# Gate rows in column groups, pool products in three passes, feature-major context keys: one layer of a hybrid diffusion block

## The chip, the core and the metric

The kernel runs on one core of a Trainium2 chip. The metric is device time in microseconds (us). The core has a matrix engine (TensorE, PE in the profile, with its weight loads as PEld), a vector engine (VectorE, DVE), a scalar engine (ScalarE, ACT), GpSimd (POOL) and SyncE (SP), which here issues most DMA transfers. Matrix products land in PSUM, eight banks of 128 x 512 floats, and ScalarE or VectorE carries them out.

## The reference

One layer with a model width of 1024 on 1024 latent tokens (a 16 x 64 grid) and 256 context tokens, all in float32:

```python
sh1, sc1, gt1, sh2, sc2, gt2 = split(silu(c) @ w_mod + b_mod, 6)       # 1024 each
h_x = rmsnorm(x, g_pre_mix) * (1 + sc1) + sh1                          # h_c: the same with c_ctx
u, q, k, v = split(h @ w_in)                                           # 512 each, for latent and context
d = window_mean(u, 2/4/8/16) - u                                       # 4 groups of 128 channels
pool = einsum('blgc,gcd->blgd', d, pool_w) * pool_scale
attn = neighbourhood_attention(q_x, k_x, v_x, k_c, v_c, rpb)           # 8 heads of 64
x = x + gt1 * rmsnorm(concat(pool, attn) @ w_out, g_post_mix)
y = square(relu((rmsnorm(x, g_pre_mlp) * (1 + sc2) + sh2) @ w1)) @ w2
out = x + gt2 * rmsnorm(y, g_post_mlp)
```

## The kernel before

A product of two float32 matrices is made in three passes: each operand is split into a high part in the type fp32r (a cast on ScalarE) and a low part (a subtraction on VectorE), and `three` (L167) adds high x high, high x low and low x high in one PSUM bank. A few small products run as plain fp32 matmuls instead; each of these shows as two records in the trace.

TensorE does the work in this order:

- Start: x is normalised and transposed, shift and scale rows are made for both token kinds (`mod_sums`, tile pm, 128x32 weights and 256 columns in four column groups of the array), and the keys kT of the latent tokens.
- Context keys and values: `pkc` is made by tokens (two groups of 24 matmuls with 512 columns), copied into kct, transposed in blocks of 128 (`pkct`, L542), and copied into kcT, feature by token. Then `pvc`, the context's values.
- The latent values `pv`, eight groups of 24.
- The pools' stage: for each of four channel groups two groups of 24 matmuls (`pu`), and `pooled` on VectorE: sums of doubling width in the pages sa and sb, edges in ed, and the difference d.
- The queries of the first half of the tokens (`pq`), then one query group of the second half, then `pool_out`: eight plain fp32 products `py` of d with pool_w, each written as a high and a low part into mix.
- Attention, 32 units (head pair j, column block m), in software-pipelined steps i: scores of unit i, transposes of unit i - 2 (`turn`), value products of unit i - 3 (`values`). The three other query groups lie between the first units.
- The output product (`out_sums`: po, then pw) begins in the steps i = 32 to 35 that run attention dry; then the MLP, two products in a scheme with seven block products, which takes the time from about 360 us on.

Four vectors are needed that come later: shift and scale of the MLP (sh, sc) and the two gates (a, b). Each is a sum on VectorE over eight loads of w_mod (`mod_sum`, L190: one operation of 128x1024 for a load), closed by a product with ones that adds the partitions. These steps are taken from a list by `background(n)`, called between the groups of matmuls. For the gates, `mod_gate` (L195) multiplies the sum by a ones matrix into all partitions (two matmuls of 512 columns), then by the norm's gain on VectorE, and one row goes to DRAM, from where `gate_page` spreads it later.

Memory is in pools with a fixed number of buffers: `act`, 33 pages of 4 KB a partition (tag pg), `wraw`, 4 buffers for loads of 512 KB, and `whl`, 8 buffers for high and low weights. A tile takes a buffer that an earlier tile gave free and waits for that tile's last reader. Where a block stands in `in_order(...)`, the listed engines keep the order as written; elsewhere a scheduler decides it. The start up to the context keys and the attention loop stand in such blocks.

In the attention loop `LOADS` and `HALVES` give the steps at which the output weights are loaded and split: at each entry of HALVES, `weight_split(n)` casts one 128x512 half on ScalarE, and `low()` subtracts it on VectorE in the next step.

Of the kernel before, what the change touches and what calls it, by code (L numbers as in the profile page):

```python
# [17 lines left out]
P = 128  # L18
# [61 lines left out]
def hybrid_block(ctx, tc, x, ctx_in, w_mod, b_mod, gp1, gp2, w_in, pool_w, rpb, w_out, w1, w2, vectors,  # L80
# [17 lines left out]
    def page(name, dt=F32):  # L98
        return act.tile([P, 1024], dt, tag="pg", name=name)
# [83 lines left out]
    def mod_sum(name, c, alloc, sT):  # L183
# [4 lines left out]
        for k in range(KT):  # L188
            w = load(f"wm{name}_{k}", w_mod[k * P : (k + 1) * P, c * D : (c + 1) * D])
            nc.vector.scalar_tensor_tensor(acc, w, sT[:, k : k + 1], acc, mul, add)  # L190
            yield acc

    def mod_gate(name, acc, gp, bank):
        g = load(f"gp{name}", gp.rearrange("(o d) -> o d", o=1).to_broadcast([P, D]).rearrange("p (a b) -> p a b", a=2))
        for h in range(2):  # L195
            hs = slice(h * 512, (h + 1) * 512)
            ps = bank(f"pg{name}{h}")
            nc.tensor.matmul(ps, ones, acc[:, hs], start=True, stop=True)
            nc.vector.tensor_tensor(acc[:, hs], ps, g[:, hs], mul)

    def mod_column(name, acc, bank):
        ps = bank(f"pc{name}")
# [20 lines left out]
    with tc.tile_pool(name="ps1", bufs=6, space=PSUM) as ps1, tc.tile_pool(name="tmp1", bufs=3) as tmp:  # L223
# [6 lines left out]
        def once(name, shape):  # L230
            return tmp.tile(shape, F32, tag=name, name=name, bufs=1)
# [300 lines left out]
        with tc.issue_after(last[ET.DVE]):  # L532
            background(4)
# [1 line left out]
        for i in range(2):  # L535
            ps = bank(f"pvc{i}")
            token_group(ps, wgt, ctx_tok(i))
            nc.scalar.copy(vcp[:, i * 512 : (i + 1) * 512], ps)
            background()
            pt = bank(f"pkct{i}")  # L540
            for j in range(4):
                nc.tensor.transpose(pt[:, j * P : (j + 1) * P], kct[:, i, j * P : (j + 1) * P], ident)  # L542
            nc.scalar.copy(kcp.rearrange("p (j i t) -> p i j t", j=4, i=2)[:, i],
                               pt.rearrange("p (j t) -> p j t", j=4))
        kc = kcp.rearrange("p (j t) -> p j t", j=4)

        vp = [page(f"v{i}") for i in range(4)]
        for m in range(NM):
# [48 lines left out]


        def pool_out(g):
            dv = dT[g].rearrange("p (r m c) -> p m r c", r=QR, m=NM)  # L600
            for b in range(2):
                ps = bank(f"py{g}_{b}")
                nc.tensor.matmul(ps, pwt[:, g, :], dv[:, 4 * b : 4 * b + 4], start=True, stop=True)
                mp = page(f"mix1_{g}", F32R) if b else wraw.tile([P, 1024], F32R, tag="raw", name=f"mix0_{g}")
                nc.scalar.activation(mp[:, :512], ps, AF.Identity, scale=pscol[:, g : g + 1])
                nc.vector.scalar_tensor_tensor(mp[:, 512:], ps, pscol[:, g : g + 1], mp[:, :512].bitcast(F32), mul, sub)
                mix[b][g] = mp

        for g in range(4):
            up = page(f"u{g}")  # L610
            for b in range(2):
                ps = bank(f"pu{g}_{b}")
                feature_group(ps, wgt, g * P, b, range(KT))
                nc.scalar.copy(up.rearrange("p (r m c) -> p m r c", r=QR, m=NM)[:, 4 * b : 4 * b + 4],
                                   ps.rearrange("p (m r c) -> p m r c", m=4, r=QR))
            dT.append(pooled(g, up))


        tabs, msk = [], []
# [41 lines left out]
            queries(j, 0, bank(f"pq{j}_0"), (1, 2, 3, 99)[j])  # L661
        mask_page()
        tables(0)
        queries(0, 1, bank("pq0_1"), 0)
        for g in range(4):
            pool_out(g)


    with (
# [117 lines left out]

        kks = (2, 3, 0, 1)
        raw_o, wo = {}, {}
        LOADS, HALVES = (8, 10, 17, 19), (12, 13, 14, 20, 21, 22, 28, 30)  # L790
        lows = []

        def high(src, hi, lo):
# [39 lines left out]
            nc.vector.tensor_tensor(mp1[t][:, hs], ps, G1[:, hs], mul)  # L833

        with in_order(ET.PE, ET.Activation, ET.DVE, ET.SP):
            queries(1, 1, bank("pq1_1"), 0)
            for i in range(N + 4):
                if i < N and units[i][1] == 2 and units[i][0] < 3:
                    tables(units[i][0] + 1)
# [11 lines left out]
                if i in HALVES:  # L851
                    weight_split(HALVES.index(i))
                if i < N:
                    scores(i)
                else:
# [524 lines left out]
```

## Time and profile before

| | us |
|---|---|
| median of three runs | 1060.99 (1060.98 to 1061.59) |
| the profiled execution | 1061.53 |
| its span, first to last instruction | 1059.7 |
| TensorE busy in it | 1045.5 |
| VectorE busy | 685.6 |
| ScalarE busy | 507.5 |
| GpSimd busy | 55.7 |

The mean granted clock of TensorE is 0.997. In a row of the timeline the first number is the start in us from the span's beginning, the second the duration; then engine, source line, operation, output tile <- input tiles, shape and count, and in brackets how long the engine sat idle before and what released it. A matmul's recorded duration overlaps the next one's, so the pace of a stream is read from start to start. A row of the chain of waits has start, length, and what ran.

### The profile page before, as it was taken

What the parts mean: (1) busy time and instruction counts of PE and PEld (TensorE: products, weight loads), DVE (VectorE), ACT (ScalarE), POOL (GpSimd) and SP (SyncE); (2) the same over time, 40 slices, a digit from 0 to 9 for tenths busy, and PEclk for the clock granted to TensorE, in tenths of its full rate; (3) what the DMA queues carried; (4) which work ended last, traced back from release to release, by engine and by line L of the source; (5) the groups of instructions that cost most, each with busy time, mean ns of one, the idle gap of its engine ahead of it and who ended that gap; (6) DMA issues with size and microseconds to landing.
All of it is one profiled execution on the core that took longest, in us unless ns stands there. A gap on an engine that the chain in (4) does not pass through costs nothing.

```text
span 1059.7 us, 15246 instructions
## 1 busy us (share of the span) xinstructions
PE 1045.5 (99%) x5870; PEld 856.4 (81%) x5870; DVE 685.6 (65%) x1071; ACT 507.5 (48%) x882; POOL 55.7 (5%) x109
## 2 busy tenths in 40 slices
PE   8999999999999999999999999999999999999996
PEld 6788888867878888888888888888888888888885
DVE  5536624846998225799987666664577666557586
ACT  7563021236998123886555454554553335334441
POOL 2020000030120003200000000000000000000001
PEclk9999999999999999999999999999999999999998
DMA  9906740531111605445745345345597666556556
GB/s 342 326 21 230 240 146 0 165 107 55 35 39 57 159 1 180 147 150 182 255 169 179 130 146 182 129 159 189 212 354 263 233 238 218 198 165 206 168 191 203
DMA packets 94268, 179.37 MB, mean 169 GB/s; under 512 B 6898, under 2 KB 39154, under 8 KB 94196
## 3 DMA queue, kind: packets, MB, share of 16 engines
q1 hardware_dynamic: 76644, 144.80, 41.6%
q10 hardware_dynamic: 16272, 29.40, 7.5%
q0 software_dynamic: 1280, 4.21, 1.1%
q8 instruction: 46, 0.75, 0.3%
q14 instruction: 26, 0.21, 0.1%
HBM read 140.62 MB, written 37.76 MB: 168 GB/s over the span
## 4 chain that ended last, share of the span: by engine, by line
PE 89%; ACT 4%; DVE 3%; issue 1%; DMA 1%; POOL 1%; SPq 0%; POOLq 0%; DVEq 0%; ACTq 0%
PE pk L400 4%; PE S L697 3%; PE pyv L170 3%; PE pyz L170 3%; PE pyx L170 3%; PE pyx L168 3%; PE phz L169 3%; PE phv L169 3%; PE phv L168 3%; PE phz L168 3%; PE pyz L169 3%; PE pyv L169 3%; PE pyv L168 3%; PE pyz L168 3%; PE phv L170 3%; PE phz L170 3%
## 5 line engine op out<-in xcount | busy, mean ns | idle before, releaser
L1029 ACT ACTIVATE c<-c 128x512 f32<-128x512 f32 x48 | 30.3, 631 | 59.9 <-DVE c L1142 23.3
L720 ACT ACTIVATE sp<-sp,nm 128x640 f32<-128x640 f32 (+1 forms) x64 | 51.4, 804 | 7.8 <-DVE nm L711 7.3
L711 DVE CUSTOM_DVE_ANT_0 sp<-S,tab 128x640 f32<-128x640 f32 (+1 forms) x56 | 42.8, 802 | 16.1 <-PE S L697 9.4
L144 DVE TENSOR_TENSOR wpS<-S,wpS 128x512 fp32r<-128x512 f32 x64 | 43.6, 686 | 11.9 <-ACT wpS L143 11.9
L170 PE MATMUL phx<-thB,wpA 128*128 128x512 f32 x128 | 49.9, 390 | 0.0
L168 PE MATMUL phx<-thB,wpA 128*128 128x512 f32 x128 | 49.9, 390 | 0.0
L169 PE MATMUL phx<-tlB,wpA 128*128 128x512 f32 x128 | 49.8, 389 | 0.0
L143 ACT CAST wpS<-S 128x512 fp32r<-128x512 f32 x64 | 39.2, 616 | 18.2 <-PE phy L170 7.8
L139 POOL TENSOR_TENSOR ry<-vy,nhalf 128x1 f32<-128x1 f32 x8 | 4.4, 550 | 600.7 <-DVE vy L137 600.7
L1030 ACT ACTIVATE c<-c 128x512 f32<-128x512 f32 x48 | 30.3, 631 | 8.1 <-DVE sa L1100 7.4
L1136 DVE TENSOR_TENSOR c<-phz,u 128x512 f32<-128x512 f32 x16 | 11.0, 690 | 32.2 <-PE phz L170 32.1
L170 PEld LDWEIGHTS phx<-thB,wpA 128*128 128x128 f32 x128 | 24.0, 188 | 5.2 <-DVE wpA L144 0.2
L697 PE MATMUL S<-kT,q 64*128 64x384 f32 (+1 forms) x128 | 27.8, 495 | 0.4 <-DVE nm L711 0.4
L168 PEld LDWEIGHTS phx<-thB,wpA 128*128 128x128 f32 x128 | 24.0, 188 | 5.0
L169 PEld LDWEIGHTS phx<-tlB,wpA 128*128 128x128 f32 x128 | 24.0, 188 | 4.9
L833 DVE TENSOR_TENSOR mp<-pw,Ga 128x512 f32<-128x512 f32 x14 | 9.6, 688 | 27.5 <-ACT jo L130 27.5
L773 PE MATMUL pa<-pt,v 128*64 128x128 f32 x352 | 25.9, 279 | 1.2 <-ACT px L753 0.6
L168 PE MATMUL phy<-thT,wpS 128*128 128x512 f32 x64 | 24.9, 389 | 0.0
L169 PE MATMUL phy<-tlT,wpS 128*128 128x512 f32 x64 | 24.9, 389 | 0.0
L170 PE MATMUL phy<-thT,wpS 128*128 128x512 f32 x64 | 24.9, 389 | 0.0
L168 PE MATMUL phz<-thT,wpS 128*128 128x512 f32 x64 | 24.9, 389 | 0.0
L169 PE MATMUL phz<-tlT,wpS 128*128 128x512 f32 x64 | 24.9, 389 | 0.0
(922 smaller groups left out, 3269.4 us busy)
## 6 DMA issues: line engine op xcount, KB each, us to landing
b<-in_w SPq DMA_DIRECT2D x64, 512.0 KB, 4.6
hrS<-hdS SPq DMA_DIRECT2D x32, 512.0 KB, 5.1
hrA<-hdA SPq DMA_DIRECT2D x24, 512.0 KB, 5.5
wm<-in_w_mod SPq DMA_DIRECT2D x16, 512.0 KB, 9.7
wa_0w<-in_w SPq DMA_DIRECT2D x16, 512.0 KB, 4.9
wa_1w<-in_w SPq DMA_DIRECT2D x16, 512.0 KB, 4.0
hdA<-c ACTq DMA_DIRECT2D x32, 256.0 KB, 2.1
hdS<-sa ACTq DMA_DIRECT2D x32, 256.0 KB, 4.4
```

What stands on the lines that cost most here:

```text
L143: nc.scalar.copy(hi, src)
L144: nc.vector.tensor_tensor(lo, src, hi.bitcast(F32), sub)
L168: nc.tensor.matmul(ps, ahi, bhi, start=first, stop=False, skip_group_check=more)
L169: nc.tensor.matmul(ps, ahi, blo, start=False, stop=False, skip_group_check=more)
L170: nc.tensor.matmul(ps, alo, bhi, start=False, stop=last, skip_group_check=more)
L400: nc.tensor.matmul(pks[b][j], wk(wgt, k, low, j * P, P), r, start=(k == 0 and n == 0), stop=(k == KT - 1 and n == 2))
L697: nc.tensor.matmul(S[e][:, c0 : c0 + keys.shape[1]], q[hs, cols], keys[hs], start=True, stop=True)
L711: nc.vector.tensor_tensor_reduce(out=to, in0=s, in1=bt, scale=1.0, scalar=BIG, op0=add, op1=ALU.min, accum_out=nm)
L720: nc.scalar.activation(sp, sp, AF.Exp, bias=least[i, e], scale=-1.0, accum_out=sums[i][:, e : e + 1])
L773: nc.tensor.matmul(pa[e * HD : (e + 1) * HD, cols], v[:, f : f + HD], turns[i][:, e, c] if c < 4 else fifths[i][:, :, (e + 1) * HD : (e + ...
L1029: nc.scalar.activation(r, src, AF.Relu)
L1030: nc.scalar.activation(r, r, AF.Square)
```

## The change

1. `mod_gate`: the gate's 1024 values are taken as four column groups of 256. Four fp32 matmuls with 32 columns of ones write to the four partition quarters of one bank, one VectorE operation of 128x256 applies the gain (loaded by four transfers), and four transfers on GpSimd's queue, in place of one on SyncE's, write the row to DRAM.
2. Context keys are made by features (four groups of 24 matmuls with 256 columns), straight into kcT's order; the copies into kct and the transposes go.
3. `background(2)` is called after each of the eight groups of the pools' stage, so the rest of gate a's and all of gate b's sums come before the queries, and so do their loads: SyncE's queue now has the last w_mod load of a, the eight of b, and both gains before the four query weight loads.
4. pool_w and the differences d are split into high and low parts (in the pools' stage), and the pools' products run in three passes. The order of TensorE is fixed around them.
5. The steps of the output weights' splits change.

```diff
     def mod_gate(name, acc, gp, bank):
-        g = load(f"gp{name}", gp.rearrange("(o d) -> o d", o=1).to_broadcast([P, D]).rearrange("p (a b) -> p a b", a=2))
-        for h in range(2):
-            hs = slice(h * 512, (h + 1) * 512)
-            ps = bank(f"pg{name}{h}")
-            nc.tensor.matmul(ps, ones, acc[:, hs], start=True, stop=True)
-            nc.vector.tensor_tensor(acc[:, hs], ps, g[:, hs], mul)
+        g = wraw.tile([P, 1024], F32, tag="raw", name=f"gp{name}w")[:, :256]
+        quarters = gp.rearrange("(c o f) -> c o f", c=4, o=1)
+        for c in range(4):
+            nc.sync.dma_start(g[32 * c : 32 * c + 32, :], quarters[c].to_broadcast([32, 256]))
+        ps = bank(f"pg{name}")
+        for c in range(4):
+            nc.tensor.matmul(ps[32 * c : 32 * c + 32, :256], ones[:, :32], acc[:, c * 256 : (c + 1) * 256],
+                             start=True, stop=True)
+        nc.vector.tensor_tensor(acc[:, :256], ps[:, :256], g, mul)
...
-                nc.sync.dma_start(gates[name], acc[0:1, :])
+                for c in range(4):
+                    nc.gpsimd.dma_start(gates[name][:, c * 256 : (c + 1) * 256], acc[32 * c : 32 * c + 1, :256])
...
         kcp = page("kcT")
-        kct = page("kct").rearrange("p (i f) -> p i f", i=2)
+        kc = kcp.rearrange("p (j t) -> p j t", j=4)
...
-        for i in range(2):
-            ps = bank(f"pkc{i}")
-            token_group(ps, wgt, ctx_tok(i))
-            if i:
+        for j in range(4):
+            ps = bank(f"pkc{j}")[:, :CTX]
+            for k in range(KT):
+                three(ps, wk(wgt, k, 0, j * P, P), wk(wgt, k, 1, j * P, P), *hc[k], k == 0, k == KT - 1)
+            if j == 3:
                 wgt = [high_low(f"wv{kk}", raw_v[kk]) for kk in range(KT // 2)]
-            nc.scalar.copy(kct[:, i], ps)
+            nc.scalar.copy(kc[:, j], ps)
...
-            pt = bank(f"pkct{i}")
-            for j in range(4):
-                nc.tensor.transpose(pt[:, j * P : (j + 1) * P], kct[:, i, j * P : (j + 1) * P], ident)
-            nc.scalar.copy(kcp.rearrange("p (j i t) -> p i j t", j=4, i=2)[:, i],
-                               pt.rearrange("p (j t) -> p j t", j=4))
...
+        pwh, pwl = (tmp.tile([P, 512], F32R, tag=f"pw{n}", name=f"pw{n}", bufs=1) for n in "hl")
...
-                nc.tensor.matmul(ps, pwt[:, g, :], dv[:, 4 * b : 4 * b + 4], start=True, stop=True)
+                hi, lo = dT[g][b]
+                gs = slice(g * P, (g + 1) * P)
+                three(ps, pwh[:, gs], pwl[:, gs], hi, lo, True, True)
...
+                if g == 1 and b == 0:
+                    with tc.issue_after(kept[ET.Activation]):
+                        split(pwt.rearrange("p g d -> p (g d)"), pwh, pwl)
+                background(2)
+            dv = pooled(g, up).rearrange("p (r m c) -> p m r c", r=QR, m=NM)
+            dT.append([])
+            for b in range(2):
+                d = page(f"d{g}_{b}", F32R)
+                hi, lo = d[:, :512], d[:, 512:]
+                bands = lambda t: t.rearrange("p (m r c) -> p m r c", m=4, r=QR)
+                split(dv[:, 4 * b : 4 * b + 4], bands(hi), bands(lo))
+                dT[g].append((hi, lo))
...
-        LOADS, HALVES = (8, 10, 17, 19), (12, 13, 14, 20, 21, 22, 28, 30)
+        LOADS, HALVES = (8, 10, 17, 19), (12, 14, 20, 22, 29, 32, 32, 33)
```

On VectorE the changed order around the last pooling groups is: gate b's multiply, wq0l, wq1l, the add into sb of the third pooling group, wq2l, the add into sa, wq3l. On ScalarE the four query weight casts stand before the copies of the last pool groups. The add into sb waits for four transfers of POOL's queue.

More of the change, by code (lines that the diff above doesn't have):

```diff
@@ L613, in hybrid_block @@
                 feature_group(ps, wgt, g * P, b, range(KT))
-                nc.scalar.copy(up.rearrange("p (r m c) -> p m r c", r=QR, m=NM)[:, 4 * b : 4 * b + 4],
-                                   ps.rearrange("p (m r c) -> p m r c", m=4, r=QR))
-            dT.append(pooled(g, up))
+                with in_order(ET.Activation) as kept:
+                    nc.scalar.copy(up.rearrange("p (r m c) -> p m r c", r=QR, m=NM)[:, 4 * b : 4 * b + 4],
+                                       ps.rearrange("p (m r c) -> p m r c", m=4, r=QR))
+                if g == 1 and b == 0:
[10 more added lines that the diff above has]
+                dT[g].append((hi, lo))
         tabs, msk = [], []
@@ L663, in hybrid_block @@
         tables(0)
-        queries(0, 1, bank("pq0_1"), 0)
-        for g in range(4):
-            pool_out(g)
+        with in_order(ET.PE) as pools:
+            queries(0, 1, bank("pq0_1"), 0)
+            for g in range(4):
+                pool_out(g)
     with (
@@ L835, in hybrid_block @@
         with in_order(ET.PE, ET.Activation, ET.DVE, ET.SP):
-            queries(1, 1, bank("pq1_1"), 0)
+            with tc.issue_after(pools[ET.PE]):
+                queries(1, 1, bank("pq1_1"), 0)
             for i in range(N + 4):
@@ L850, in hybrid_block @@
                     mixed_split(i // 8 - 1, 0)
-                if i in HALVES:
-                    weight_split(HALVES.index(i))
+                for n, at in enumerate(HALVES):
+                    if at == i:
+                        weight_split(n)
                 if i < N:
```

2 lines of the change are left out of this document (removed).

## The prediction, on record before the changed kernel ran

> **What bounds the kernel now.** I read the page first, then busy time by stage (the windows), then what TensorE waited for, and last the timeline of TensorE at each place that the change touches.
>
> ```profile
> span 1059.7 us, 15246 instructions
> PE 1045.5 (99%) x5870; PEld 856.4 (81%) x5870; DVE 685.6 (65%) x1071; ACT 507.5 (48%) x882; POOL 55.7 (5%) x109
> PE 89%; ACT 4%; DVE 3%; issue 1%; DMA 1%; POOL 1%; SPq 0%; POOLq 0%; DVEq 0%; ACTq 0%
> ```
>
> TensorE is 89% of the chain. By stage (us; then PE, PEld, DVE, ACT, POOL busy; granted clock, DMA share, GB/s):
>
> ```profile
> 146.65:190.20 43.55, 43.55 (x194) 36.07 (x193) 19.57 (x44) 8.85 (x13) 0.00 (x0) 1.00 0.15 48
> 190.20:233.14 42.94, 42.94 (x169) 31.24 (x168) 28.43 (x38) 9.73 (x15) 12.56 (x30) 1.00 0.50 165
> 233.14:341.70 108.56, 106.91 (x1490) 85.62 (x1489) 89.18 (x260) 89.39 (x233) 10.41 (x24) 1.00 0.12 36
> 341.70:358.45 16.75, 16.75 (x146) 13.27 (x145) 5.51 (x14) 4.57 (x13) 0.00 (x0) 1.00 0.84 240
> ```
>
> The rows are the pools' stage, the queries with the pools' products, attention, and the last units with the first output products. In the first two TensorE never stops at full clock while VectorE is about half idle. So work taken off TensorE there is time saved, and work put on VectorE and ScalarE is free until one of their results comes too late. Only attention loads all three engines, and there TensorE's recorded waits are small:
>
> ```profile
> PE pa L773 <- ACT px L753: 0.6, 3, 0.2
> PE S L697 <- DVE nm L711: 0.4, 1, 0.4
> ```
>
> The last column is the longest single wait. All stages after 233 us start from what TensorE and its helpers finished before, so a saving ahead of them moves them all.
>
> **The change, part by part.** Context keys first. TensorE's timeline:
>
> ```profile
> 76.58 0.39 PE L168 MATMUL pkc<-wk0h,hc 128*128 128x512 f32 x1
> ...
> 87.46 0.39 PE L168 MATMUL pvc<-wv0h,hc 128*128 128x512 f32 x1
> ...
> 92.90 0.60 PE L542 MATMUL pkct<-ident,kct 128*128 128x128 f32 x4
> ...
> 93.57 0.39 PE L169 MATMUL pvc<-wv0l,hc 128*128 128x512 f32 x1
> ```
>
> Between the first two rows lie 48 matmuls in 10.88 us, 0.2267 each. Four transposes and the one matmul after them take 0.67 (92.90 to 93.57), so the transposes cost 0.67 - 0.23 = 0.44, twice: 0.89. Removed: 10.88 + 0.89 = 11.77. Added: 96 matmuls with 256 moving columns in place of 512. No fp32r matmul of that width is in the trace. Its neighbours:
>
> ```profile
> 70.71 1.91 PE L460 MATMUL pct<-ident,c 128*128 128x128 f32 x16
> 72.38 0.47 PE L400 MATMUL pk<-hx,wk2h 128*128 128x512 f32 x1
> ```
> ```profile
> L204 PEld LDWEIGHTS pcsh<-ones,accsh x16: 188/192/192, 110.0 to 111.7; 128*128 128x128 f32 x16
> L204 PE MATMUL pcsh<-ones,accsh x16: 164/250/250, 110.2 to 111.8; 128*128 128x1 f32 x16
> ```
>
> Sixteen 128-wide transposes take 1.67, 0.104 each; sixteen records of a single column start from 110.2 to 111.8, 0.107 each. Both load 128x128 weights every time, so about 0.106 is the floor that a weight load leaves. A line from (128 columns, 0.104) to (512, 0.2267) gives 0.145 at 256, an upper bound if the floor does not bind alone. Half of the 512-wide row is 0.1133. I take a little over half, 0.1165, because it lies above the floor and part of 0.2267 may be fixed: 96 x 0.1165 = 11.18, a gain of 0.59 (bounds 10.2 to 13.9, a gain of 1.6 to a loss of 2.1).
>
> A rule of the Trainium skill speaks against this step: TensorE: Matmul & The Clock Gate, Part 3, "What overlaps and what doesn't", says that a weight load overlaps running matmuls only when its row groups differ; here all 128 rows are the same. By it each pair would cost load plus stream, some 0.107 + 0.107, and the 96 would take 20.5, a loss of 8.8. By that rule the 512-wide pairs would need about 0.32, and the trace has 0.2267: it disagrees.
>
> Gates. Rows of the chain, then TensorE around a product in column groups:
>
> ```profile
> 206.52 1.72 PE pga L198 x4
> 219.17 1.72 PE pgb L198 x4
> 220.89 6.87 PE py L603 x16
> ```
> ```profile
> 27.10 0.63 PE L400 MATMUL pk<-hx,wk0h 128*128 128x512 f32 x2
> 27.66 1.93 PE L351 MATMUL pm<-wm,sT 128*32 128x256 f32 x32
> 29.53 0.73 PE L400 MATMUL pk<-hx,wk0h 128*128 128x512 f32 x2
> ```
>
> Removed: 2 x 1.72 = 3.44. Added: twice four fp32 matmuls of form 128x32 weights and 256 columns, each in its own group. The L351 rows are that form in four groups: 16 matmuls in 29.53 - 27.66 = 1.87, 0.47 per round of four. Before them two pk matmuls take 0.56 rather than 0.45; I count that change of form 0.11 on both sides. So 0.68 a gate, 1.36 in all: a gain of 2.08 (2.5 with nothing for the form; 0 if a lone round does not run abreast, since four times 0.43, py's 6.87 / 16, is again 1.72).
>
> Pools' products: 16 records, 6.87, become 24 fp32r matmuls of 0.2267, 5.44: a gain of 1.43. Their evictions end later than the products, covered by the query group of 5.44 behind them.
>
> What this puts on the helpers:
>
> ```profile
> 193.44 1.28 DVE L190 SCALAR_TENSOR_TENSOR acca<-wma_7w,sx,acca 128x1024 f32<-128x1024 f32 x1
> 345.76 0.68 DVE L795 TENSOR_TENSOR mix<-f,mix 128x512 fp32r<-128x512 f32 x1
> 342.45 0.61 ACT L794 CAST mix<-f 128x512 fp32r<-128x512 f32 x1
> ```
>
> Nine sums move into the pools' stage (9 x 1.28 = 11.5), and nine splits are new (6.1 on VectorE, 5.5 on ScalarE). VectorE there goes from 19.6 to about 38 of 43.6, ScalarE from 8.9 to 14.4. It fits, but the next results to come late are the split weights:
>
> ```profile
> 185.93 1.05 ACT L143 CAST wq0h<-wq0w 128x1024 fp32r<-128x1024 f32 x1 [0.50 <-PE pu L169]
> 188.37 1.23 DVE L144 TENSOR_TENSOR wq1l<-wq1w,wq1h 128x1024 fp32r<-128x1024 f32 x1
> 191.09 1.23 DVE L144 TENSOR_TENSOR wq3l<-wq3w,wq3h 128x1024 fp32r<-128x1024 f32 x1
> 181.23 1.23 DVE L576 TENSOR_TENSOR sb<-sa 128x1021 f32<-128x1021 f32 x1
> ```
> ```profile
> acca<-in_b_mod POOLq DMA_DIRECT2D x1, 4.0 KB, 3.4
> accb<-in_b_mod POOLq DMA_DIRECT2D x1, 4.0 KB, 1.7
> 201.82 0.49 POOL L186 DMA_DIRECT2D accb<-in_b_mod  x1 [0.29 <-POOL accb L185]
> ```
> ```profile
> 78.71 0.43 DVE L180 TENSOR_TENSOR hc<-hc7t,hc 128x256 fp32r<-128x256 f32 x1 [0.48 <-ACT hc L176]
> ```
>
> The context keys meet two such edges. Their first group reads all eight hc tiles in 2.8 us instead of 5.4: the low part of hc7 is ready at 79.14 and read by the 23rd matmul, 76.58 + 22 x 0.1165 = 79.14. And the values' weights take over buffers that the last of the four groups still reads: the first is free 78 matmuls on, 85.7; cast (1.05) and subtraction (1.23) end at 88.0, and the second value matmul, 76.58 + 96 x 0.1165 + 0.23, reads it at 88.0. I put 0.1 on both (0 to 0.3).
>
> The query weights: now wq3l ends at 192.32 and is first read by the 21st matmul from 190.20 on, 194.73: 2.4 us of slack. In the changed order the last pooling group stands between: wq1l, the add sb, wq2l, the add sa, wq3l. Four times some 1.19 behind 189.60 is 194.35; the slack is 0.4. And sb takes over the page of gate b's sum, so it waits for the four row transfers that POOL now issues. The fourth pool group's last products start at 184.75 (146.65 + 7 x 5.44); gate b's product is just ahead, its multiply (128x256, as the hc row) 0.4, then four issues of about 0.5, so the last starts near 187.1 and lands 1.7 to 3.4 later, at 188.8 to 190.5, against 189.60. Behind sb wait wq2l and wq3l, and TensorE behind them: 0 to 0.5 of stall on this count. I take 0.2, with 1.2 as the upper end if the transfers share the queues with the last query weight load, which now also starts only after gate b's multiply.
>
> Last units. Casts leave units 13, 21, 28 and 30; one comes to 29 and three to 32 and 33.
>
> ```profile
> 343.73 0.32 ACT L753 COPY px<-pa 128x192 f32<-128x192 f32 x1 [0.66 <-PE pz L739]
> 344.12 0.88 PE L773 MATMUL pa<-pt,v 128*64 128x128 f32 x12
> 350.60 0.39 PE L169 MATMUL po<-wo_1l,mix 128*128 128x512 f32 x1
> ```
>
> Behind the cast at 342.45 ScalarE is free 0.66 before px. Two more casts take 1.0 to 1.2, so px and the value product behind it come 0.3 to 0.5 later. wo_1l's last half is ready about 350.6, when it is read (350.60): 0.1. I count +0.35 (0 to 0.9). What attention can gain from four casts less is bounded by its 1.0 of recorded waits; I take 0.1.
>
> Sum: -0.59 + 0.1 - 2.08 - 1.43 + 0.2 + 0.35 - 0.1 = **-3.55**. The profiled execution took 1061.53 us (its span 1059.7 and 1.8 around it), 0.54 above the median of 1060.99. From the median: **1057.4**; such a profile would have a span near 1056.
>
> **Rivals.** *Weight loads set the pace of the context keys (slower).*
>
> ```profile
> 76.58 0.19 PEld L169 LDWEIGHTS pkc<-wk0l,hc 128*128 128x128 f32 x1
> ```
>
> This load starts with the matmul ahead of it (76.58), takes 0.19, and the next matmul starts at 0.2267, right behind. If that chain is what sets 0.2267, halving the columns halves nothing: 96 x 0.2267 = 21.76, a loss of 9.99, and with the other terms (-2.96) +7.0: 1068. It decides from 0.175 a matmul on, where the other gains are gone and 2.1 lost. Against it: the pcsh loads take 192 ns as well, yet follow each other at 0.11. I give it 7%.
>
> *Query weights late.* If the gate rows land 2 to 3 us later than I count, sb holds wq2l and wq3l for that long and TensorE stops 2 to 3 us: 1059.3 to 1060.3, within the noise of no change at the end. POOL's 4 KB transfers spread from 1.7 to 3.4, which speaks for it; VectorE idling for the first cast while POOL issues speaks against. 12%. The Trainium skill, SBUF — State Buffer, "The DVE blocks DMA trap", says that POOL cannot write descriptors while VectorE runs a fast-mode copy; if that held for these subtractions the transfers would land this late. The accb transfer above, at 1.7, ran beside an idle VectorE and doesn't tell.
>
> *The column groups don't run abreast for a single round*: gates stay at 3.44 and the sum is -1.5: 1059.5. The L351 rows speak against; 5%.
>
> **Numbers.** A measurement of this kernel can tell about 0.2%, 2.1 us, from no change. The forecast case has 73% and spreads over 1055.8 to 1058.8 by its bounds; the two milder rivals 17% (1059 to 1060.3), the slow one 7%, and 3% for losses that I don't see. The range 1055.8 to 1060.2 leaves out the slow rival, the unseen and a tail. Faster: nearly all of the forecast case and a share of the mild rivals, 0.78; within 0.2%: 0.13; slower: 0.09.
>
> **What would show it.** Context-key matmuls 0.113 to 0.12 apart and no transposes; pga and pgb near 0.5 to 0.7; py's stretch 5.4; no TensorE gap over 0.5 in the query group that follows the pools; values of unit 29 delayed by under 0.5. It is wrong if the context keys take over 13.9 us, if TensorE waits more than 1.2 us for wq2l or wq3l, or if anything behind 358 us changes length.

## The result, and the profile after

| | before | changed |
|---|---|---|
| median of eight runs each, us | 1061.14 (1060.98 to 1061.59) | 1057.96 (1057.71 to 1058.13) |
| the profiled execution | 1061.53 | 1057.97 |
| its span | 1059.7 | 1056.1 |

The changed kernel is 3.18 us faster, a ratio of 0.9969 (95% interval 0.9959 to 0.9980). The forecast was 1057.4 in a range of 1055.8 to 1060.2. The first lines of the page, and then the windows of the changed kernel: context keys, context values, the pools' stage, the queries with the pools' products, attention, last units (us; then PE, PEld, DVE, ACT, POOL busy; clock, DMA share, GB/s).

```profile
span 1056.1 us, 15402 instructions
PE 1041.4 (99%) x5926; PEld 857.4 (81%) x5926; DVE 687.7 (65%) x1078; ACT 510.2 (48%) x891; POOL 59.5 (6%) x117
```
```profile
76.45:88.03 11.58, 11.58 (x97) 11.55 (x96) 2.27 (x4) 7.09 (x15) 0.00 (x0) 1.00 0.00 0
88.03:99.11 11.08, 11.08 (x51) 9.01 (x49) 8.78 (x8) 2.67 (x4) 1.44 (x2) 1.00 0.80 276
146.32:191.44 45.12, 45.12 (x209) 36.20 (x208) 29.07 (x46) 10.92 (x17) 3.82 (x8) 1.00 0.49 155
191.44:229.63 38.19, 38.19 (x169) 31.29 (x167) 21.71 (x43) 11.79 (x20) 7.21 (x19) 1.00 0.13 37
229.63:337.71 108.08, 106.56 (x1489) 85.64 (x1489) 87.41 (x258) 88.06 (x231) 14.36 (x34) 1.00 0.12 38
337.71:355.04 17.33, 17.18 (x146) 13.12 (x145) 7.21 (x16) 5.94 (x16) 0.00 (x0) 1.00 0.76 218
```

TensorE is still busy for all of the first four stages. From the first pool projection to the first scores it was 86.63 us (146.51 to 233.14) and is 83.31. Attention is 0.48 shorter (108.56 before), the last units are 0.58 longer (16.75 before). Behind them nothing moved: the first matmul of the MLP came 3.31 earlier, counted from the first context key, and that of its last product, 439 us on, also 3.31. From the last matmul's start to the end of the trace it is 8.27 us in place of 8.50; with the same code there the other traces have 8.11 to 9.03.

TensorE's timeline at the context keys: the first matmul, the only irregular step among the 96, and the context values behind them.

```profile
76.45 0.28 PE L168 MATMUL pkc<-hc,wk0h 128*128 128x256 f32 x1
...
79.08 0.37 PE L169 MATMUL pkc<-hc,wk3h 128*128 128x256 f32 x1
79.29 0.28 PE L170 MATMUL pkc<-hc,wk3l 128*128 128x256 f32 x1
...
88.03 0.39 PE L168 MATMUL pvc<-wv0h,hc 128*128 128x512 f32 x1
88.31 0.50 PE L169 MATMUL pvc<-wv0l,hc 128*128 128x512 f32 x1
88.65 0.39 PE L170 MATMUL pvc<-wv0h,hc 128*128 128x512 f32 x1
```

From 79.29 to 88.03 there are 73 matmuls, 0.1197 each. The matmul at 79.08 takes 0.21 to the next: it read hc7's low part, the wait that was counted. The first two context values take 0.28 and 0.34 in place of 0.2267, the wait for wv0l. Now the gate's product and the pools' products:

```profile
156.97 0.39 PE L170 MATMUL pu<-hx,wu3l 128*128 128x512 f32 x1
157.29 0.64 PE L201 MATMUL pga<-acca,ones 128*32 128x256 f32 x8
157.86 0.50 PE L168 MATMUL pu<-hx,wu0h 128*128 128x512 f32 x1
158.20 0.39 PE L169 MATMUL pu<-hx,wu0h 128*128 128x512 f32 x1
...
218.66 0.39 PE L168 MATMUL py<-d,pwh 128*128 128x512 f32 x1
...
224.10 0.39 PE L168 MATMUL pq<-hx,wq0h 128*128 128x512 f32 x1
```

The gate takes 0.57 for its eight records, and the steps on its two sides 0.32 and 0.34 in place of 0.2267, so 0.57 + 0.09 + 0.11 = 0.78. The 24 products of the pools take 5.44, without a gap.

### The profile page after: what moved, and what is told of

It is laid out like the page before. It is cut to its first block, busy times and chain, and to the rows that moved or that the text cites. A ratio compares the mean times of both kernels' runs of the same rounds, so it can differ in the third digit from the quotient of the medians.

```text
span 1056.1 us, 15402 instructions
## 1 busy us (share of the span) xinstructions
PE 1041.4 (99%) x5926; PEld 857.4 (81%) x5926; DVE 687.7 (65%) x1078; ACT 510.2 (48%) x891; POOL 59.5 (6%) x117
## 4 chain that ended last, share of the span: by engine, by line
PE 82%; issue 11%; ACT 3%; DVE 2%; POOL 1%; DMA 1%; SPq 0%; POOLq 0%; DVEq 0%; ACTq 0%
PE pk L404 4%; PE pyv L169 3%; PE pyv L168 3%; PE pyz L169 3%; PE pyz L168 3%; PE pyx L169 3%; PE phv L170 3%; PE phz L170 3%; PE pyx L170 3%; PE phv L168 3%; PE phz L168 3%; PE phv L169 3%; PE phz L169 3%; PE pyx L168 3%; PE pyv L170 3%
```

## The experiments

Each is the changed kernel with one edit. "Against before" is the median less that of the kernel before in the same comparison (1061.83, 1061.45, 1061.63 and 1061.56 us in the four); the changed kernel's is -3.18.

| run | median us | against before | ratio (95% interval) |
|---|---|---|---|
| keys_by_tokens | 1058.64 | -3.19 | 0.9971 (0.9961 to 0.9982) |
| keys_in_pairs | 1058.25 | -3.20 | 0.9968 (0.9956 to 0.9981) |
| gates_whole | 1060.01 | -1.82 | 0.9983 (0.9974 to 0.9992) |
| gates_one_strip | 1060.84 | -0.61 | 0.9997 (0.9988 to 1.0006) |
| pools_plain | 1060.24 | -1.59 | 0.9985 (0.9977 to 0.9994) |
| sums_in_queries | 1078.75 | +17.30 | 1.0161 (1.0147 to 1.0174) |
| plain_sums_in_queries | 1060.44 | -1.19 | 0.9991 (0.9981 to 1.0000) |
| sums_in_queries_own | 1066.86 | +5.30 | 1.0051 (1.0034 to 1.0068) |
| rows_on_sync | 1058.64 | -2.99 | 0.9972 (0.9961 to 0.9982) |
| casts_as_before | 1057.80 | -4.03 | 0.9963 (0.9949 to 0.9977) |
| casts_spread | 1058.49 | -2.96 | 0.9974 (0.9965 to 0.9983) |
| pairs_casts_28_29 | 1058.03 | -3.60 | 0.9967 (0.9955 to 0.9980) |

The intervals are some 2 us wide. For edits of a few tenths I read stage lengths from the traces: in kernels that are the same up to the first context key, that matmul started anywhere from 76.45 to 78.01 us, but up to the first scores, and again in the last units, the same stretch of the same code repeats within 0.05. Attention does not: in the ten traces with the changed kernel's attention it lasts 107.82 to 108.37, so there I read single units.

**Context keys.** keys_by_tokens puts the `token_group` loop, kct and the transposes back. keys_in_pairs keeps the features-first form:

```diff
-        for j in range(4):
-            ps = bank(f"pkc{j}")[:, :CTX]
+        for js in ((0, 1), (2, 3)):
+            pss = [bank(f"pkc{j}")[:, :CTX] for j in js]
             for k in range(KT):
-                three(ps, wk(wgt, k, 0, j * P, P), wk(wgt, k, 1, j * P, P), *hc[k], k == 0, k == KT - 1)
+                for ps, j in zip(pss, js):
+                    three(ps, wk(wgt, k, 0, j * P, P), wk(wgt, k, 1, j * P, P), *hc[k], k == 0, k == KT - 1)
```

> The changed kernel with only the context keys put back: 48 matmuls of 512 columns for the token groups, eight transposes, two casts of them. Theory A (what the trace of the change reads like): the halved matmul keeps a fixed part of about 0.013 us, 96 of them cost 0.7 more than 48 of 512 columns, and the two waits at the edges (0.1 in the first group, 0.17 at the context values) eat the rest of the 0.89 that the transposes and their wait cost, so that the whole edit was worth 0.07. Then the pool projections start 69.93 us after the first context-key matmul instead of 69.87, and the time is 1057.8 to 1058.3. Rival B (the size that was forecast, 0.59 less 0.1): the time is 1058.4 to 1058.6. Under both the stages behind keep their lengths.

> The changed kernel with the context keys' four groups in two pairs, the features outermost within a pair, so that the last context page (hc7) is needed 48 matmuls after the first and not 24, and the first weights' buffers come free earlier for the value weights. Theory A: the edit's gain was eaten by a fixed part of each halved matmul (96 times 0.0063, which stays) and by waits at the edges (0.1 for hc7, 0.17 at the context values, which go): from the first context key to the first context value 11.47 instead of 11.58, the context values 0.17 shorter, so 0.25 to 0.3 from the first context key to the first pool projection. Rival B: the two waits are steps of the weights' load on TensorE and not waits for data: nothing changes, 69.87 again. Rival C: two banks open side by side cost something: over 69.87.

With the keys by tokens, the pool projections start 69.93 us after the first context key, in the changed kernel 69.87 (69.85 to 69.90 in the other traces with its context keys): the edit is worth 0.03 to 0.08, theory A. In pairs it is 69.63, 0.24 less, theory A again. The windows of keys_in_pairs (context keys, context values):

```profile
77.02:88.53 11.51, 11.51 (x97) 11.51 (x96) 4.00 (x6) 7.87 (x14) 0.00 (x0) 1.00 0.06 18
88.53:99.44 10.91, 10.91 (x51) 9.02 (x49) 8.51 (x7) 2.18 (x4) 1.44 (x2) 1.00 0.89 314
```

11.51 is 96 x 0.1197 and 0.02 over, and 10.91 is 48 x 0.2267. So both waits were for data and can be had back; the pace of 0.1197 stays.

**Gates.** gates_whole goes back to two matmuls of 512 columns with 128 columns of ones; gates_one_strip keeps the small products but writes all four to rows 0 to 31 of two banks (the gain's load and its multiplies change to 32 rows with it):

```diff
-            nc.tensor.matmul(ps[32 * c : 32 * c + 32, :256], ones[:, :32], acc[:, c * 256 : (c + 1) * 256],
-                             start=True, stop=True)
+            nc.tensor.matmul(ps[:32, c * 256 : (c + 1) * 256], ones[:, :32],
+                             acc[:, h * 512 + c * 256 : h * 512 + (c + 1) * 256], start=True, stop=True)
```

> The changed kernel with the gates' products put back to two matmuls of 128 rows by 512 columns each (the gate row is still stored through GpSimd, the multiplier page is one load of 128 x 1024). Theory A: the four column groups of the changed kernel ran abreast, each gate took 0.78 us of TensorE with its edges instead of 1.72, so this run is 1.9 us longer, 1059.6 to 1060.1, and all of it lies where the two products stand, among the pool projections. Rival B: part of the gain came from the shorter load and store, not from TensorE: then the two products take 1.72 each again but a stage behind them changes its length too, and the time is off 1059.8 by over 0.5.

> The changed kernel with each gate's four products of 32 rows by 256 columns all in the same 32 columns of TensorE (rows 0 to 31 of two banks), one after the other, instead of in four groups of 32. The work of each product is the same, only the group differs. Theory A: what made the gate cheap is that the four groups run abreast; then eight passes of some 0.215 us stand one behind the other, each gate takes 1.72 again, and the run is 1.9 us longer than the changed kernel (the pool projections last 47.05 us instead of 45.12). Rival B: the small tile itself is the cheap thing, abreast or not; then each gate stays at about 0.78, and the projections last 45.1 to 45.3.

gates_whole: the pools' stage lasts 47.05 (45.12 in the changed kernel), 1.93 more, and the stages behind it are as they were (38.17, 108.07 and 17.33): theory A. gates_one_strip: 47.65, 2.53 more: theory A, and 0.6 beyond its size. TensorE's timeline, first of gates_one_strip, then of gates_whole:

```profile
157.84 1.91 PE L200 MATMUL pga<-acca,ones 128*32 128x256 f32 x8
159.68 0.50 PE L168 MATMUL pu<-hx,wu0h 128*128 128x512 f32 x1
```
```profile
157.60 1.88 PE L199 MATMUL pga<-acca,ones 128*128 128x512 f32 x4
158.91 0.79 PE L168 MATMUL pu<-hx,wu0h 128*128 128x512 f32 x1
```

The same eight records take 1.84 in one strip and 0.57 in four. The small tile alone isn't cheap, it is even dearer than the whole product; that the four run abreast is the whole gain, also in a lone round.

**Pools' products, and where the sums stand.** pools_plain multiplies in plain float32 and splits nothing; sums_in_queries takes out `background(2)`, so the last sums and both gates come among the queries as they did before; plain_sums_in_queries does both; sums_in_queries_own is sums_in_queries with gate b's sum in a tile of its own.

```diff
-                background(2)
```
```diff
-        rest.append(mod_row("b", 5, gp2))
+        rest.append(mod_row("b", 5, gp2, lambda n: once(n, [P, 1024])))
```

> The changed kernel with the pools' products in plain float32 again: eight matmuls in two passes, no split of the pooled pages and of the pool weights. Theory A: the products' stretch is 6.87 us instead of 5.44, and the splits cost nothing where they stand, so the time is 1.43 longer, 1059.2 to 1059.6. Rival B: the splits, eight casts on ScalarE and eight subtractions on VectorE in the pools' stage, hold something up that the trace does not show as a gap of TensorE (the query weights, the pooled pages); then the stretch grows by 1.43 but the query groups get shorter, and the time is under 1059.1.

> The changed kernel without the background sums in the pools' stage, so that the gates' last sums and products stand among the query groups again, as they did before the change. Theory A: where the gates stand is worth nothing, since VectorE has room in both stages and TensorE waits in neither; the pool projections and queries together last as long as in the changed kernel (83.3 us from the first projection to the first scores), and the time is 1057.8 to 1058.4 on the chip of the first comparison. Rival B: in the query groups the sums come ahead of the query weights' splits on VectorE, and TensorE waits there: 0.4 to 1.5 slower, with a gap of TensorE ahead of a pq group that VectorE ends. Rival C: the other way about, the sums among the pools had delayed the pooled pages or the weights by something that shows as no gap: faster by over 0.3.

> The changed kernel without the background sums in the pools' stage and with the pools' products in plain float32, so that no pooled page is split; the context keys and the gates' column groups stay. Sums among the queries alone made the changed kernel some 17 us slower, with TensorE waiting for the second gate's sums. Theory A: the two edits hang together: the split pages of the pools (eight more pages, and their subtractions on VectorE ahead of the sums) are what makes the sums late among the queries; without them the sums are done in time, no gap opens, and this kernel is as long as the one with plain pools, 1.4 to 2.0 slower than the changed kernel and 1 to 2 faster than the kernel before. Rival B: the place of the sums alone costs it (the order written out for the pools' products, or the wider place of the gates' products): then TensorE waits here too, and the kernel is at least 10 slower than the kernel before.

> The kernel with the sums among the queries (17 us slower than the changed kernel), with one thing more: the second gate's running sum has a tile of its own instead of one of the 33 shared pages. In the trace of the slow kernel GpSimd cleared that page only at 212.73, released by a query group's last matmul, and the second gate's sums ran from 223.5 to 236, with TensorE waiting for them. Theory A: it was the page: the split pooled pages hold eight, and the sum got one only when a query group gave up its latents. With a tile of its own the sums run from about 193.5 to 207, while VectorE sat idle 13.6 there; the wait for the second gate goes, and what is left is the third and fourth pools' averages, which stand behind the first gate's multiply at 207 and end some 6 later than in the changed kernel: 0 to 4 slower than the changed kernel. Rival B: it was VectorE's order, with the first gate's multiply waiting for TensorE at its head: the sums stay late, and the kernel stays 10 to 17 slower.

pools_plain: the queries and products last 39.66 in place of 38.19, 1.47 more, theory A; attention is 0.28 longer, all of it in unit 15, which no run explains. sums_in_queries fell outside all three theories: from the first pool projection to the first scores 102.79 in place of 83.31. By the medians it is 17.3 slower than the kernel before and some 20.5 slower than the changed kernel; the two expectations that say 17 slower than the changed kernel are off by that. The wait of TensorE ("issue": the profile names no releaser), the rows of VectorE and of GpSimd around gate b, and the window of the gap:

```profile
PE pgb L201 <- issue: 16.1, 1, 16.1
```
```profile
207.12 0.42 DVE L203 TENSOR_TENSOR acca<-pga,gpaw 128x256 f32<-128x256 f32 x1 [13.64 <-PE pga L201]
223.53 1.28 DVE L190 SCALAR_TENSOR_TENSOR accb<-wmb_0w,sx,accb 128x1024 f32<-128x1024 f32 x1
```
```profile
212.73 0.95 POOL L185 MEMSET accb<- 128x1024 f32 x1 [2.98 <-PE pq L170]
```
```profile
219.76:236.06 16.30, 0.15 (x1) 0.03 (x1) 13.54 (x21) 3.10 (x6) 0.94 (x3) 0.58 0.40 137
```

GpSimd could clear accb only when a query group gave up its latents' page; VectorE, which had idled 13.64, by then had the third and fourth pools' averages ahead in its order, so the sums ran from 223.53 and gate b's product, ahead of the pools' products on TensorE, waited 16 us. With plain products (eight pages fewer) the same order of sums costs nothing: 43.52 + 41.20 = 84.72 from projection to scores, against 84.78 in pools_plain. So the splits of the pools' products and the sums' early place hang together. The page alone is not all: with a tile of its own the sum gives back 11.4 of the 19.5 (91.41), not the 15.5 or more that theory A asked for, and by the medians it is 8.5 slower than the changed kernel, between theory A's 4 and rival B's 10. The rest, 8.1, lies in shorter waits of TensorE (3.1 for gate a's multiply, 1.0 for gate b's, 0.8 and 1.2 for ScalarE's copies) and in what follows them:

```profile
226.31 0.79 PE L168 MATMUL py<-d,pwh 128*128 128x512 f32 x1 [1.23 <-ACT q L669]
226.90 0.63 PE L169 MATMUL py<-d,pwh 128*128 128x512 f32 x1
227.32 0.63 PE L170 MATMUL py<-d,pwl 128*128 128x512 f32 x1
```
```profile
226.31:229.03 2.72, 2.72 (x6) 2.14 (x7) 0.95 (x2) 2.48 (x5) 1.04 (x4) 0.50 0.29 64
```

After those pauses the granted clock is 0.50 for 2.72 us and a matmul takes 0.43 in place of 0.2267.

**The queue of the gate rows.** rows_on_sync:

```diff
-                    nc.gpsimd.dma_start(gates[name][:, c * 256 : (c + 1) * 256], acc[32 * c : 32 * c + 1, :256])
+                    nc.sync.dma_start(gates[name][:, c * 256 : (c + 1) * 256], acc[32 * c : 32 * c + 1, :256])
```

> The changed kernel with the gate rows' eight stores issued by SyncE instead of GpSimd. The second gate's four stores then stand ahead of the last query weights' load in SyncE's order and wait for VectorE's multiply, which ended at 186.4 us in the trace of the changed kernel; the load was issued there at 186.45. Theory A: the load is issued some 1.5 us later, its split still finds its turn on VectorE (which began at 194.58, some 3 us after the page could be split), and the time is the changed kernel's, within 0.3. Rival B: the split gets later by what the load does, and TensorE waits for it in the first query group: 1 to 1.5 slower, with a gap at the wq3 matmuls.

```profile
187.05 1.12 SPq L501 DMA_DIRECT2D gb<-accb  x4
188.22 0.39 SPq L148 DMA_DIRECT2D wq3w<-in_w_in  x1
```

Counted from the first context key, the last query weights are asked for 1.2 us later, and the two stages last 45.12 and 38.17: nothing lost, theory A.

**Casts of the output weights.** Three other lists of HALVES; the last one with the context keys in pairs.

```diff
-        LOADS, HALVES = (8, 10, 17, 19), (12, 14, 20, 22, 29, 32, 32, 33)
+        LOADS, HALVES = (8, 10, 17, 19), (12, 13, 14, 20, 21, 22, 28, 30)     # casts_as_before
+        LOADS, HALVES = (8, 10, 17, 19), (9, 10, 13, 17, 18, 21, 25, 26)      # casts_spread
+        LOADS, HALVES = (8, 10, 17, 19), (12, 13, 14, 20, 21, 22, 28, 29)     # pairs_casts_28_29
```

> The changed kernel with the output weights' casts of the first half back at units 12, 13, 14, 20, 21, 22, 28 and 30. Theory A (from the periods of the units in both traces): a cast costs nothing at 13 and 21, some 0.15 to 0.2 at 28, 29 and 30, and three casts at the last units cost 0.58 from the first output sums to the second half's; what the attention gained is 0.2 from units 28 to 30 and, by another cause, 0.28 at units 5 and 7. So this kernel gives back the 0.58 and loses 0.2: 0.35 to 0.4 faster, 1057.4 to 1057.8. Rival B: the whole gain of 0.48 in the attention is the casts': then the move is worth nothing in sum, and the time is 1057.9 to 1058.1. Rival C: the tail's 0.58 has another cause (a load or a bank): the attention gets longer by 0.2 to 0.5, the tail stays, and the time is 1058.2 to 1058.5.

> The changed kernel with the output weights' eight casts at units 9, 10, 13, 17, 18, 21, 25 and 26, all of them units in which ScalarE was busy for 0.45 to 1.0 us less than the unit lasted in the trace of the changed kernel (2.07 of 3.08 at unit 9, 2.32 of 2.85 at unit 10, 2.56 of 3.20 at unit 13). Theory A: a cast of 0.61 us costs what ScalarE lacks of room in its unit; then these cost nothing or little, units 12, 14, 20, 22 and 29 last 3.20, the attention is 0.6 to 0.9 shorter than in the changed kernel, and the 0.58 at the last units is gone as well: 1.1 to 1.5 faster in all. Rival B: it is the place in ScalarE's order that costs, ahead of the exponentials, wherever there is room at other times of the unit: each costs 0.15 to 0.2 in a row's first unit, and the attention is as long as in the changed kernel or longer; only the 0.58 is gone. Rival C: VectorE's subtraction of 0.68 in the next unit costs instead (at 10, 11, 18, 19, 26, 27, beside the tables at 18 and 19): attention longer by up to 1.

> The changed kernel with the context keys in two pairs and the output weights' casts at units 12, 13, 14, 20, 21, 22, 28 and 29. Theory A: the pairs give 0.24 as in their own run; no cast at the last units gives 0.58; against the changed kernel's attention the casts at 13 and 21 cost nothing, as the second of a row, and that at 28 costs 0.2 with nothing at 29, against 0.14 now: 0.06 more, and 0.25 for unit 7's state, which came with the casts as they were before. In sum 0.5 to 0.8 faster than the changed kernel, 3.6 to 4.0 faster than the kernel before. Rival B: 29 costs 0.14 again behind 28: 0.4 to 0.6 faster than the changed kernel.

casts_as_before: attention 108.30, last units 16.74. ScalarE at the last units, changed kernel, then casts_as_before:

```profile
338.42 0.62 ACT L809 CAST mix<-f 128x512 fp32r<-128x512 f32 x1
338.94 0.63 ACT L809 CAST wo_0h<-wor 128x512 fp32r<-128x512 f32 x1
339.45 0.63 ACT L809 CAST wo_1h<-wor 128x512 fp32r<-128x512 f32 x1
339.97 0.33 ACT L768 COPY px<-pa 128x192 f32<-128x192 f32 x1
```
```profile
339.47 0.60 ACT L809 CAST mix<-f 128x512 fp32r<-128x512 f32 x1
340.73 0.32 ACT L768 COPY px<-pa 128x192 f32<-128x192 f32 x1 [0.66 <-PE pz L754]
```

Two casts fill the 0.66 and push px 0.24 further (2.26 behind the first output product in place of 2.02); with that the last units are 0.58 to 0.59 longer. Together attention and last units take 125.04 in place of 125.41, 0.37 less. That is theory A's sum, but not by its terms: the casts at 28 to 30 cost 0.06 over units 28 to 31 where 0.2 was counted. The rest of the 0.22 that attention lost stands in unit 7 (0.27 more), units 14 and 15 (0.13 more) and 18 to 20 (0.25 less), and these differ by as much between kernels with the same casts. The 0.59 of the last units is shown; that undoing this part gains some 0.5 in all is argued from the units.

casts_spread put every cast into a unit where ScalarE had room, and attention grew to 109.00, 0.92 more. Unit 7 has 0.29 of it, and no cast stands there (more on it under Attention below). Units 10, 18 and 26 are 0.28, 0.24 and 0.28 longer. ScalarE's copy px and the value products that read it in unit 10, first in the changed kernel without a cast, then here:

```profile
269.43 0.21 ACT L768 COPY px<-pa 128x64 f32<-128x64 f32 x1
269.81 0.66 PE L788 MATMUL pa<-pt,vc 128*64 128x128 f32 x8
```
```profile
270.06 0.61 ACT L809 CAST wo_2h<-wor 128x512 fp32r<-128x512 f32 x1
270.57 0.21 ACT L768 COPY px<-pa 128x64 f32<-128x64 f32 x1
270.83 0.66 PE L788 MATMUL pa<-pt,vc 128*64 128x128 f32 x8 [0.21 <-ACT px L768]
```

In the changed kernel px begins 1.45 after the unit's first scores (267.98), here 1.85 (268.72), directly behind the cast. TensorE waits 0.21 for it, its only recorded wait in the unit, and the unit lasts 3.14 in place of 2.85; units 18 and 26 show the same wait (0.25 and 0.21). VectorE's 2.45 in the changed kernel's unit 10 and the subtraction's 0.68 would also make 3.13, which is theory C, but units 11, 19 and 27, with a subtraction and no cast, last 3.01, 3.02 and 3.00 (3.15, 2.98 and 3.14 in the changed kernel). The casts at 9, 17 and 25 cost nothing: px still begins at 1.45. So a cast costs time where ScalarE has no room ahead of px, whatever room it has later in the unit. Rival B, the place in ScalarE's order, comes nearest, though not in a row's first unit as it said. Only the last units came back to 16.75.

pairs_casts_28_29: the stretch from the first context key to the values is 0.24 shorter, attention 108.13, last units 16.75; to the first matmul of the MLP it is 0.76 ahead of the changed kernel, of which 0.28 is lost in the MLP (308.95 in place of 308.67, also seen in gates_one_strip; its cause is open). Its median is 3.60 under the kernel before, where the changed kernel's is 3.18, and the profiled spans are 1056.0 and 1056.1. That is the lower end of theory A's 0.5 to 0.8 at the end of the trace (0.49) and just under it by the medians (0.42). It lies in rival B's 0.4 to 0.6 as well. Units 28 and 29 last 3.39 and 3.20, so the cast at 29 cost nothing, theory A; but unit 7, for which theory A counted 0.25, stayed at 3.02, and the loss in the MLP stands in its place. It is ahead of both kernels, of the changed one by less than the medians' interval.

## Why the prediction was right

| step | forecast | both traces | with the part undone |
|---|---|---|---|
| context keys and their two edges | -0.49 | -0.07 | 0.06 |
| gates | -2.08 | -1.88 | 1.93 |
| pools' products | -1.43 | -1.43 | 1.47 |
| query weights late | +0.2 | 0 | |
| attention | -0.1 | -0.48 | |
| last units | +0.35 | +0.58 | |

The second column adds up to -3.28; at the MLP's first matmul it is -3.31. Two steps carried the total, gates and pools' products, and these were right in mechanism and size. That the others' misses of +0.42, -0.20, -0.38 and +0.23, and +0.20 at the gates, nearly cancel is luck. Of the signs named, all came: 0.12 between context keys, 0.57 for a gate, 5.44 for the products, no gap in the query group behind them, unit 29's values 0.22 later, no other length behind 358 us up to the last matmul.

*Context keys.* The step that failed is "I take a little over half, 0.1165". From 0.2267 at 512 columns and 0.1197 at 256, half of the columns save 0.107, and on a line through the two 0.0127 is there at either width; 96 x (0.1197 - 0.1165) = 0.31. The edges were the right two and took 0.26 (0.09 at hc7, 0.17 at the values) in place of 0.1. The transposes and the steps behind them, 0.96 in place of 0.89, give 0.07 back. The Trainium skill, TensorE: Matmul & The Clock Gate, "Wait — 56ns, not 53.3ns?", gives start-to-start as columns by 2.4 GHz plus about 2.5 ns: the slope agrees (106.7 ns for 256 columns), the fixed part here is five times that. What it is was not separated; the weight loads, busy 11.55 of 11.58 here, are not ruled out as a part of it. The slow rival is ruled out.

*Gates.* 0.78 in place of 0.68 each: the edges cost 0.20, where 0.11 had been taken off both sides of a run of 16. The rival of column groups that don't run abreast is ruled out; gates_one_strip shows what it would have cost.

*Query weights.* TensorE did not stall, but the wait that was feared was there, on VectorE. The rows of GpSimd's four stores (the line under them is for the same four) and of VectorE in the changed kernel, then VectorE's add in rows_on_sync:

```profile
186.71 1.91 POOL L501 DMA_DIRECT2D gb<-accb  x4 [26.09 <-DVE accb L203]
DMA to landing us min/median/max: 2.8/3.3/3.8
```
```profile
191.11 1.22 DVE L577 TENSOR_TENSOR sb<-sa 128x1021 f32<-128x1021 f32 x1
192.32 1.22 DVE L144 TENSOR_TENSOR wq2l<-wq2w,wq2h 128x1024 fp32r<-128x1024 f32 x1
194.58 1.22 DVE L144 TENSOR_TENSOR wq3l<-wq3w,wq3h 128x1024 fp32r<-128x1024 f32 x1
```
```profile
191.52 1.22 DVE L577 TENSOR_TENSOR sb<-sa 128x1021 f32<-128x1021 f32 x1
```

The order is the one that was read from the diff. The last store was issued at 188.14 and landed at 190.99, and the add into sb began at 191.11, 0.33 ahead of the first query matmul (191.44). In rows_on_sync it is 0.52 ahead (192.04), so the stores held it by 0.19. (Against the first query matmul the landing is at 189.6 on the time scale of the kernel before, within the 188.8 to 190.5 that was counted, and not 2 to 3 us later, as the rival had it.) wq3l then ends at 195.8, and the 21st matmul from 191.44 on reads it at 191.44 + 20 x 0.2267 = 195.97. The order alone leaves a slack of 0.36 (0.4 was counted); the stores took 0.19 of it, and the 0.17 that was left kept TensorE from waiting. In casts_spread they took 0.07; in the other traces with this order on VectorE they landed in time.

*The place of the sums.* "It fits" was right for the new place. VectorE was busy for 29.1 of 45.1 us in the pools' stage where 38 was counted, since only five of the nine new splits came ahead of the queries. (In the queries' stage of the kernel before it was a third idle, 28.43 of 42.94 busy, and not about half.) What the prediction didn't see is that the old place no longer would fit: with the split pages it is 18 us dearer than with plain products (102.79 against 84.72).

*Last units.* The mechanism was right (px 0.24 later, where 0.3 to 0.5 was counted), the size 0.23 short: the value products of unit 29 came 0.22 later, two low halves of the weights 0.11 each, and the rest is smaller steps.

*Attention.* "What attention can gain from four casts less is bounded by its 1.0 of recorded waits; I take 0.1" missed 0.38, and the bound did not hold: recorded waits are still 0.9 in the changed kernel, and the gains came in units for which the traces record no wait of TensorE. Units 28 to 30 give 0.20 (9.94 before, 9.74 after) and are the casts'; the casts that left 13 and 21 gave nothing, and the last unit lost 0.14 (3.34, as in casts_spread, which has no cast near it). Unit 5 gives 0.14: in the one trace of before VectorE pauses for 0.23 there, in none of the 13 others, and why is open. Unit 7 gives 0.27, and that is not the change's doing: gates_whole and sums_in_queries, with the changed kernel's attention, have the long unit 7 too (3.27 and 3.29). It is which of two operations began first. VectorE's copy and GpSimd's first table operation, before, then changed, then casts_as_before:

```profile
263.00 0.50 DVE L726 COPY rb<-ri 128x128 f32<-128x128 f32 x1
262.96 1.26 POOL L641 TENSOR_TENSOR tab<-msk,U 128x128 f32<-128x128 f32 x3 [30.06 <-DVE ri L724]
```
```profile
259.35 0.23 DVE L741 COPY rb<-ri 128x128 f32<-128x128 f32 x1
259.38 1.32 POOL L655 TENSOR_TENSOR tab<-msk,U 128x128 f32<-128x128 f32 x3 [25.89 <-DVE ri L739]
```
```profile
260.13 0.50 DVE L741 COPY rb<-ri 128x128 f32<-128x128 f32 x1
260.09 1.27 POOL L655 TENSOR_TENSOR tab<-msk,U 128x128 f32<-128x128 f32 x3 [26.01 <-DVE ri L739]
```

In all 14 traces of this case the copy takes 0.48 to 0.51 where GpSimd began 0.02 to 0.05 ahead of it (five traces) and 0.23 where the copy began first (nine). The Trainium skill, SBUF — State Buffer, "SBUF: two separate sides", says that of VectorE and GpSimd the one that begins first holds their shared port pair for its whole instruction, for VectorE operations in a mode with two ports or with two inputs from SBUF. The order of beginning agrees; that this copy, with one input, runs in such a mode is not shown here, and it lost 0.26 to 0.28 where GpSimd's 0.45 still had 0.40 to 0.43 to run.

## What to carry to other kernels

A small fp32 product on a full TensorE is worth cutting into four column groups even when it stands alone, and halving a matmul's columns halves its time only up to a fixed part, so twice as many matmuls must save something else as well. Where VectorE has room by its share, ask for pages and for order too: a sum that waits for a page stands behind what arrived first. A cast is free only where ScalarE has room ahead of the copy that TensorE waits for; the room in the whole unit doesn't tell. When a total of a few us is met, check its terms one by one, since here five misses of 0.2 to 0.4 cancelled and one gain of 0.27 was a tie that fell the other way.

## What was not expected of the hardware

A lone round of four column groups takes 0.57 for what one group does in 1.84. An fp32r matmul takes 0.2267 at 512 columns and 0.1197 at 256, which is 0.0063 more than half. In sums_in_queries_own TensorE paused 3.1, 0.8, 1.0 and 1.2 us within 20 us, and the granted clock was 0.50 over the next 2.72 us. A lead of 0.02 to 0.05 us of GpSimd over VectorE goes with a 128x128 copy of 0.48 to 0.51 in place of 0.23 us, and with a unit of 3.27 to 3.31 in place of 3.02.
